# Matmuls of ones in three norm gaps, and late low parts of h in the first product behind a norm

## The chip, the cores and the metric

The kernel runs on one core of one Trainium2 chip. The metric is device time in microseconds (us) of one execution; lower is better. Engines are named as in the profile: PE (TensorE matmuls) and PEld (its weight loads), DVE (VectorE), ACT (ScalarE), POOL (GpSimd), SP (SyncE, which issues the DMAs). The granted clock of TensorE stands at one of two levels, 2.4 GHz (a granted share of 1.0) and 1.2 GHz (0.5); a stretch that saw both shows a value between.

## The reference

A decoder trunk of four layers on x (256 tokens, 1024 features, float32). Each layer has a token mixer (layers 0 and 3 a gated MLP, layer 1 latent attention, layer 2 a gated recurrence) and a convolutional feed-forward part, each behind a norm and a modulation by a conditioning vector:

```python
for i in range(DEPTH):                       # 4
    mod = c_act @ ada_w[i] + ada_b[i]
    sh1, sc1, g1, sh2, sc2, g2 = jnp.split(mod, 6, axis=-1)
    h = modulate(rmsnorm(x, mix_norm_g[i]), sh1, sc1)
    y = mixer(h)                             # by i % 3
    x = x + (1.0 + g1)[:, None, :] * y
    h = modulate(rmsnorm(x, ffn_norm_g[i]), sh2, sc2)
    x = x + (1.0 + g2)[:, None, :] * conv_ffn(h, ff_w_up[i], ...)
return rmsnorm(x, final_g)
```

## The kernel before, in words

Every large product is done with split operands: a weight tile `raw` comes by DMA, ACT casts it to its high part `wh` (L210), DVE subtracts to get the low part `wl` (L213); the activations h are split in the same way into `hh` (cast on ACT, L599) and `hlo` (subtraction on DVE, L600). A product of two such operands is three matmuls (`mm3`, L243 to L245): high by high, high by low, low by high. h lies with features on the partitions, in 8 chunks of 128 features (the K chunks) by 256 tokens.

A *unit* is one weight tile of 1 MB. The up-projection of a feed-forward part (`ffn`) has 22 units, each a `proj_pair`: two output blocks g of 128 features, 8 K chunks, three matmuls of 256 columns each, so 48 matmuls. The first unit behind a norm is called with `outer=True` (in the ffn for c = 0, in `mla` for the pair `cq`, in `hgrn` for the first `hf`): the loop over K chunks is the outer one, so that the product can start when the first chunk of h is there.

Between two products stands a *norm gap*. The last unit of a product (`out_end`) finishes four accumulators one after the other; `residual` adds each to x (DVE, L522, L523) and squares it (ACT, L525); `root` gives the scale per token; `scaled` multiplies x by it into `gx` (L467 for the first 128 tokens, L469 and L470 for the other 128). Then `turned` transposes `gx` on PE into PSUM tiles `xt` (16 transposes of 128x128, L478), and `modulate_chunk` makes each of the 8 chunks: DVE multiplies and adds into `nt` (L487), ACT casts `hh`, DVE subtracts `hlo`. The order of `gx`'s two halves matters: the transposes of a chunk's first 128 tokens need L467, those of the second need L469.

The gaps are named here by what follows them: ffn 0, MLA (the mixer of layer 1), ffn 1, HGRN (the mixer of layer 2), ffn 2, the mixer of layer 3, ffn 3. In some of them small matmuls `adaps<-adaw,cact` of the conditioning vectors are put on PE (`pace`, `GAPS`, `pacing`).

Float32 matmuls of one 128x128 tile with another stand elsewhere too: the program starts with 12 such matmuls of ones (`warmup`, L1253), and each unit of the gated MLP has four (`sv`, L768: two blocks by two halves of the tokens).

The order on each engine is fixed when the program is built: a scheduler lists the instructions, and can set matmuls of the second unit between those of the first; each engine then works through its list in order, waiting on semaphores. `tc.issue_after(i)` makes an instruction stand behind i in that list.

Of the kernel before, what the change touches and what calls it, by code (L numbers as in the profile page):

```python
# [21 lines left out]
P = 128  # L22
# [4 lines left out]
NRAW = 5  # L27
GAPS = [3, 2, 4, 3, 5, 3, 3, 0]
GAPW = 7
GAPBIG = 4  # L30
LAST = 2
GCH = 6
# [59 lines left out]
def build(ctx, tc, A, out, stages=None):  # L92
    nc = tc.nc
    pe, act, dve, pool = nc.tensor, nc.scalar, nc.vector, nc.gpsimd
# [21 lines left out]
    def acc(name, shape=(P, 512)):  # L116
        return pp.tile(list(shape), F32, tag="acc", name=name, bufs=4)
# [29 lines left out]
    onesw = one.tile([P, P], F32, name="ones")  # L147
# [6 lines left out]
    i = act.activation(cact[:], cin[:], AF.Silu)  # L154
# [18 lines left out]
    state = {"dma": 0, "conv": 0, "use": 0, "ahead": 2, "chain": (), "left": 99, "tag": "raw", "p": 0.0, "d": 0.0, "gap": 0, "rate": {"p": 0.0, "d": 0.0}}  # L173
# [18 lines left out]
    def conv_half():  # L192

        if not halves:
            if state["dma"] == state["conv"]:
                if state["dma"] == len(plan):
                    return
                dma_next()
            raw, n = raws.pop(0)
            ready.append([])  # L200
            halves.extend((raw, o, min(1024, n - o), state["conv"]) for o in range(0, n, 1024))
            state["conv"] += 1
        raw, o, w, n = halves.pop(0)
        wh = wp.tile([P, 1024], F32R, tag="wh", name=f"wh{n}_{o}", bufs=5)
        wl = wp.tile([P, 1024], F32R, tag="wl", name=f"wl{n}_{o}", bufs=5)
        with contextlib.ExitStack() as es:

            for ins in state["chain"]:
                es.enter_context(tc.issue_after(ins))
            act.copy(wh[:, :w], raw[:, o : o + w])  # L210
            if "sub1" in state:
                es.enter_context(tc.issue_after(state["sub1"]))
            i = dve.tensor_tensor(wl[:, :w], raw[:, o : o + w], wh[:, :w].bitcast(F32), op=ALU.subtract)  # L213
            state["sub"] = getattr(i, "ins", i)
        ready[-1].append((wh, wl))

    def unit(ahead=None, more=DMA_AHEAD):
        u = state["use"]
        ahead = state["ahead"] if ahead is None else ahead
        while state["dma"] < min(len(plan), u + ahead + (more if u else 0)):  # L220
            dma_next()
        while state["conv"] < min(len(plan), u + ahead) or halves:
            conv_half()
        state["use"] += 1
        r = ready.pop(0)
        pacing()
        return r
# [9 lines left out]
    def hl(parts, o, n):  # L237

        i, r = divmod(o, 1024)
        return parts[i][0][:, r : r + n], parts[i][1][:, r : r + n]  # L240

    def mm3(ps, lh, ll, rh, rl, start, stop):
        pe.matmul(ps, lh, rh, start=start, stop=False)  # L243
        pe.matmul(ps, lh, rl, start=False, stop=False)  # L244
        i = pe.matmul(ps, ll, rh, start=False, stop=stop)  # L245
        state["mm"] = getattr(i, "ins", i)
        return i
# [141 lines left out]
    def ada_load(m):  # L389
        if todo[m]:  # L390
            loaded[m].append((state["use"], todo[m].pop(0)(), state["tag"] == "big"))

    def ada_run(m):
        if not loaded[m]:
            ada_load(m)
        if loaded[m]:
            loaded[m].pop(0)[1]()
            owner[m].pop(0)

    def flush(upto=None, mid=0):  # L400
        for e in list(late):
            if e[0] - mid < state["use"] if upto is None else e[2] <= upto:
                late.remove(e)
                e[1]()

    def need(l, u):

        for m in "pd":
            while owner[m] and min(owner[m]) <= (l, u):
                ada_run(m)  # L410
        flush((l, u))

    def pacing():
# [6 lines left out]
        for m in "pd":  # L420
            while loaded[m] and loaded[m][0][0] + 2 <= state["use"] and not (m == "p" and left <= GAPW):
                ada_run(m)
        for m in "pd":
            if left > (GAPW if m == "p" else 2):
                state[m] += state["rate"][m]
                while state[m] >= 1:
                    state[m] -= 1
                    ada_load(m)
        if left <= GAPW and len(loaded["p"]) < state["gap"]:
            tag, state["tag"] = state["tag"], "big" if sum(e[2] for e in loaded["p"]) < GAPBIG else "raw"  # L430
            ada_load("p")
# [38 lines left out]
        i = act.activation(xn[:, 512:D], x[:, t, 512:D], AF.Copy, scale=rs)  # L470
        state["chain"] += (getattr(i, "ins", i),)

    def turned(c, w, bank=misc):

        ps = bank("xt", (P, w, S))
        for e in range(w):
            for t in range(2):
                pe.transpose(ps[:, e, t * P : t * P + P], cur["gx"][:, t, (c + e) * P : (c + e) * P + P], ident[:])  # L478
        return ps
# [4 lines left out]
    def modulate_chunk(l, which, c, xt):  # L484
        b = 24 * which + c
        t = t1("nt")
        i = dve.tensor_scalar(t[:], xt, amul[:, l, which, c : c + 1], mod[:, l, b : b + 1], op0=ALU.mult, op1=ALU.add)  # L487
        h, lo = split(hh[:, c, :], hlo[:, c, :], t[:])
        return getattr(i, "ins", i), h

    def modulated(l, which):
        tiles = [(0, 1), (1, 2), (3, 2), (5, 2), (7, 1)]

        late = misc if which == 0 and l % 3 == 0 else acc
        xts = [turned(*i) for i in tiles[:3]]
        while loaded["p"]:
            ada_run("p")
        need(l, 1 + 3 * which)
        for i, (c0, w) in enumerate(tiles):
            if 0 < i < 3:  # L500
                xts.append(turned(*tiles[i + 2], late))
            for c in range(c0, c0 + w):
                ins = modulate_chunk(l, which, c, xts[i][:, c - c0, :])
                if c < 2:
                    state["chain"] += ins
                if c in CONVAT:
                    conv_half()
# [111 lines left out]
    def proj_pair(src_h, src_l, nk, name, outer=False):  # L619

        w = unit()
        ps = acc(name, (P, 2, S))
        if outer:
            for k in range(nk):
                for g in range(2):
                    a, b = hl(w, (g * nk + k) * P, P)
                    mm3(ps[:, g, :], a, b, src_h(k), src_l(k), k == 0 and g == 0, k == nk - 1 and g == 1)
            return ps
        for g in range(2):
            for k in range(nk):  # L630
                a, b = hl(w, (g * nk + k) * P, P)
                mm3(ps[:, g, :], a, b, src_h(k), src_l(k), k == 0, k == nk - 1)
            if g == 0:
                flush(mid=1)
        return ps
# [183 lines left out]
    def mla(l):  # L819
# [3 lines left out]
        qr = tables.pop()  # L823
        kr, cs, sn = (qr[:, i, :] for i in (4, 5, 6))
        ps_q = proj_pair(hk, lk, KC, "cq", KOUT > 0)
        cq = t2("cq", (P, 2, S))
        act.copy(cq[:], ps_q[:])
# [440 lines left out]
    for kind, l in stages:  # L1268
# [3 lines left out]
        if kind == "mix":  # L1272
# [3 lines left out]
            if l % 3 == 0:  # L1276
                if quick:
# [4 lines left out]
                    def start(chunk):  # L1282
                        for step in FIRST.split():
                            if step == "d":
                                dma_next()
                                continue
                            if step == "p":
                                with tc.issue_after(state["lastdma"]):
                                    nc.sync.dma_start(prm[:, n0:n1], A["prm"][:, n0:n1])
                                conv_load(l)  # L1290
                                late_c()
                                continue
                            c = int(step[1])
                            if step[0] == "a":
                                if c % 2 == 0:
                                    xt[0] = turned(c, 2)
                                if c:
                                    ada_first(l, c)
                                first_store(l, c)
                                state.setdefault("sub1", modulate_chunk(l, 0, c, xt[0][:, c % 2, :])[0])  # L1300
                            else:
                                chunk(c)

                    gmlp(l, l // 3, start)
                else:
                    modulated(l, 0)
                    gmlp(l, l // 3)
            elif l == 1:
                modulated(l, 0)
                mla(l)  # L1310
            else:
                modulated(l, 0)
                hgrn(l)
# [99 lines left out]
```

## Time and profile before

| | us |
|---|---|
| median of three runs (1352.07 to 1353.33) | 1353.07 |
| the profiled execution | 1353.27 |
| its span, first to last instruction | 1351.2 |
| PE busy | 1316.6 |
| DVE busy | 1112.7 |
| ACT busy | 773.5 |
| mean granted clock of TensorE | 0.993 |

The profiled execution spent 2.07 us outside its span. The profile lists when each instruction started, how long it took, and what ended the idle time before it. Matmuls overlap: each row lasts longer than the distance to the next row, and the distance is the price.

### The profile page before, as it was taken

The page shows a single profiled execution, that of the slowest core. Times are in us where ns is not written, and L with a number is a line of the kernel's source. Part 1 is how long each engine was busy: PE and PEld are TensorE (multiplying, and loading weights), DVE is VectorE, ACT ScalarE, POOL GpSimd, SP SyncE. Part 2 cuts the span into 40 slices and gives each one's busy share as a digit, 9 for nine tenths or more (in the row PEclk, how much of TensorE's full clock was granted, in tenths as well). Part 3 has the DMA queues.
Part 4 walks back from the last instruction along what each step waited for, and adds up shares of the span by engine and source line. Part 5 has one row for each costly group of instructions (what it writes and reads, how often), then busy time and mean ns, then how long its engine had stood idle before and what let it go on. Part 6 is the DMA issues. An engine that isn't in the chain of part 4 may idle for free.

```text
span 1351.2 us, 24627 instructions
## 1 busy us (share of the span) xinstructions
PE 1316.6 (97%) x10092; PEld 1192.5 (88%) x10092; DVE 1112.7 (82%) x1818; ACT 773.5 (57%) x1212; POOL 17.3 (1%) x27
## 2 busy tenths in 40 slices
PE   8999989999989999999999999999999999999997
PEld 6799789998777799998897879999878998899986
DVE  5699788888888789999889988988985964888854
ACT  3764366665366566654675647665455644666643
POOL 0100000000000000000000000000001000000000
PEclk8999999999999999999999999999999999999999
DMA  9868945557986466498675575558977445254550
GB/s 378 349 235 318 403 185 187 213 193 267 424 333 244 172 219 244 166 360 359 236 295 190 219 305 189 214 192 317 369 297 259 168 166 216 98 204 179 198 197 32
DMA packets 49160, 330.68 MB, mean 245 GB/s; under 512 B 6548, under 2 KB 7572, under 8 KB 10134
## 3 DMA queue, kind: packets, MB, share of 16 engines
q1 hardware_dynamic: 47888, 327.40, 63.7%
q10 hardware_dynamic: 1160, 1.71, 0.4%
q8 instruction: 79, 1.29, 0.4%
q14 instruction: 33, 0.27, 0.1%
HBM read 328.01 MB, written 1.08 MB: 244 GB/s over the span
## 4 chain that ended last, share of the span: by engine, by line
PE 85%; DVE 9%; ACT 3%; issue 1%; DMA 1%; ACTq 0%; DVEq 0%
PE up L245 12%; PE up L243 12%; PE up L244 12%; PE dn L243 5%; PE dn L245 5%; PE dn L244 5%; PE u L244 2%; PE u L243 2%; PE u L245 2%; DVE wl L213 2%; PE v L243 2%; PE v L244 2%; PE v L245 2%; PE go L243 2%; PE go L244 2%; PE go L245 2%
## 5 line engine op out<-in xcount | busy, mean ns | idle before, releaser
L210 ACT CAST wh<-raw 128x1024 fp32r<-128x1024 f32 x418 | 432.8, 1048 | 324.0 <-PE up L244 110.9
L213 DVE TENSOR_TENSOR wl<-raw,wh 128x1024 fp32r<-128x1024 f32 x418 | 507.2, 1225 | 84.6 <-ACT wh L210 83.8
L245 PE MATMUL up<-hh,wl 128*128 128x256 f32 x1408 | 397.8, 283 | 0.9 <-DVE wl L213 0.9
L243 PE MATMUL up<-hh,wh 128*128 128x256 f32 x1408 | 397.7, 284 | 0.0
L244 PE MATMUL up<-hlo,wh 128*128 128x256 f32 x1408 | 397.3, 283 | 0.1
L245 PEld LDWEIGHTS up<-hh,wl 128*128 128x128 f32 x1408 | 270.4, 192 | 1.3 <-DVE wl L213 1.3
L243 PEld LDWEIGHTS up<-hh,wh 128*128 128x128 f32 x1408 | 270.0, 192 | 0.6 <-issue 0.4
L244 PEld LDWEIGHTS up<-hlo,wh 128*128 128x128 f32 x1408 | 270.1, 192 | 0.3 <-DVE hlo L600 0.3
L349 DVE CUSTOM_DVE_ANT_0 adaw<-adaw,cbc,prm 128x1024 f32<-128x1024 f32 x120 | 151.3, 1282 | 0.3 <-DMA adaw<-adad 0.3
L244 PE MATMUL dn<-wl,gh 128*128 128x512 f32 x352 | 137.0, 389 | 0.0
L245 PE MATMUL dn<-wh,gl 128*128 128x512 f32 x352 | 136.8, 389 | 0.0
L243 PE MATMUL dn<-wh,gh 128*128 128x512 f32 x352 | 134.7, 390 | 0.5 <-DVE y L1217 0.5
L1215 ACT ACTIVATE y<-up,cwb 128x256 f32<-128x256 f32 x176 | 99.0, 562 | 58.1 <-DVE y L1217 57.9
L1216 DVE SCALAR_TENSOR_TENSOR y<-up,cwb,y 128x255 f32<-128x255 f32 x176 | 84.5, 480 | 34.0 <-ACT y L1215 33.5
L1217 DVE SCALAR_TENSOR_TENSOR y<-up,cwb,y 128x254 f32<-128x254 f32 x176 | 84.1, 478 | 1.5
L243 PEld LDWEIGHTS dn<-wh,gh 128*128 128x128 f32 x352 | 66.0, 188 | 15.2 <-issue 1.7
L245 PEld LDWEIGHTS dn<-wh,gl 128*128 128x128 f32 x352 | 66.1, 188 | 13.7
L244 PEld LDWEIGHTS dn<-wl,gh 128*128 128x128 f32 x352 | 66.1, 188 | 13.5
L243 PE MATMUL u<-hh,wh 128*128 128x256 f32 x256 | 74.0, 289 | 0.0
L245 PE MATMUL u<-hh,wl 128*128 128x256 f32 x256 | 72.4, 283 | 0.0
L244 PE MATMUL u<-hlo,wh 128*128 128x256 f32 x256 | 72.4, 283 | 0.0
L600 DVE TENSOR_TENSOR gl<-g,gh 128x256 fp32r<-128x256 f32 x88 | 37.1, 421 | 22.1 <-ACT gh L599 20.5
(332 smaller groups left out, 2060.4 us busy)
## 6 DMA issues: line engine op xcount, KB each, us to landing
raw<-up SPq DMA_DIRECT2D x88, 1024.0 KB
adaw<-adad SPq DMA_DIRECT2D x60, 1024.0 KB
raw<-dn SPq DMA_DIRECT2D x44, 1024.0 KB
adaw<-adap SPq DMA_DIRECT2D x28, 1024.0 KB
raw<-gmu SPq DMA_DIRECT2D x16, 1024.0 KB
raw<-gmo SPq DMA_DIRECT2D x16, 1024.0 KB
raw<-gmv SPq DMA_DIRECT2D x15, 1024.0 KB
adaf<-ada SPq DMA_DIRECT2D x8, 1024.0 KB
```

Source lines behind the costliest of these rows:

```text
L210: act.copy(wh[:, :w], raw[:, o : o + w])
L213: i = dve.tensor_tensor(wl[:, :w], raw[:, o : o + w], wh[:, :w].bitcast(F32), op=ALU.subtract)
L243: pe.matmul(ps, lh, rh, start=start, stop=False)
L244: pe.matmul(ps, lh, rl, start=False, stop=False)
L245: i = pe.matmul(ps, ll, rh, start=False, stop=stop)
L349: r = dve.tensor_tensor_reduce(raw[:, e, :], raw[:, e, :], cbc[:], 1.0, prm[:, c0 : c0 + 1], ALU.mult, ALU.add, mod[:, l, b : b + 1])
L600: b = dve.tensor_tensor(lo, src, h.bitcast(F32), op=ALU.subtract)
L1215: act.activation(y[:], ps[:, e, :], AF.Identity, bias=b, scale=w[2])
L1216: dve.scalar_tensor_tensor(y[:, 1:], ps[:, e, : S - 1], w[1], y[:, 1:], op0=ALU.mult, op1=ALU.add)
L1217: dve.scalar_tensor_tensor(y[:, 2:], ps[:, e, : S - 2], w[0], y[:, 2:], op0=ALU.mult, op1=ALU.add)
```

## The change

Two edits. First, `turned` gets a parameter `fill`: ahead of the transposes of the first tile it issues that many plain matmuls of a 128x128 tile of ones with itself (float32), into the PSUM tile that the transposes then overwrite, and held behind the last matmul of the product (`state["mm"]`). `modulated` asks for 30 in the gap of ffn 0, 30 in that of MLA, 24 in that of ffn 3, none elsewhere. Second, in the first unit behind a norm the matmuls with `hlo` of a K chunk are issued two K chunks later than those with `hh`. No arithmetic on the data is added or dropped.

```diff
+FILL = [30, 30, 0, 0, 0, 0, 24]
...
-    def turned(c, w, bank=misc):
+    def turned(c, w, bank=misc, fill=0):
+
         ps = bank("xt", (P, w, S))
+        with contextlib.ExitStack() as es:
+            if fill:
+                es.enter_context(tc.issue_after(state["mm"]))
+            for i in range(fill):
+                pe.matmul(ps[:, 0, :P], onesw[:], onesw[:], start=True, stop=True)
...
-        xts = [turned(*i) for i in tiles[:3]]
+        xts = [turned(*i, fill=0 if j else FILL[2 * l + which - 1]) for j, i in enumerate(tiles[:3])]
...
         if outer:
-            for k in range(nk):
-                for g in range(2):
+            for k in range(nk + 2):
+                for g in range(2) if k < nk else ():
                     a, b = hl(w, (g * nk + k) * P, P)
-                    mm3(ps[:, g, :], a, b, src_h(k), src_l(k), k == 0 and g == 0, k == nk - 1 and g == 1)
+                    pe.matmul(ps[:, g, :], a, src_h(k), start=k == 0 and g == 0, stop=False)
+                    pe.matmul(ps[:, g, :], b, src_h(k), start=False, stop=False)
+                for g in range(2) if k > 1 else ():
+                    a = hl(w, (g * nk + k - 2) * P, P)[0]
+                    i = pe.matmul(ps[:, g, :], a, src_l(k - 2), start=False, stop=k == nk + 1 and g == 1)
+            state["mm"] = getattr(i, "ins", i)
             return ps
```

On PE, in the gap of ffn 0, this stood before: the end of the product `go`, the transposes, the first unit.

```order
L244 MATMUL go_1503<-wl_1024_1739,yh_868 128x512
L245 MATMUL go_1503<-wh_1024_1738,yl_869 128x512
L478 MATMUL xt<-ident,gx 128x128 x16
L243 MATMUL up_1931<-hh,wh_0_1759 128x256
L244 MATMUL up_1931<-hlo,wh_0_1759 128x256
```

And this stands there now (the lines of the file have moved by a few):

```order
L245 MATMUL go_1503<-wl_1024_1739,yh_868 128x512
L246 MATMUL go_1503<-wh_1024_1738,yl_869 128x512
L482 MATMUL xt<-ones 128x128 x30
L485 MATMUL xt<-ident,gx 128x128 x16
L635 MATMUL up_1961<-hh,wh_0_1759 128x256
L636 MATMUL up_1961<-hh,wl_0_1760 128x256
```

The 30 matmuls stand between the product and all 16 transposes, so no transpose can run before the last of them. The gaps of MLA (x30) and ffn 3 (x24) read the same.

On PE, the beginning of ffn 1, whose gap has no matmuls of ones, before (`up_5090` is the first unit, `up_5162` the second; `wh_0` and `wh_1024` are the two output blocks of a unit):

```order
L243 MATMUL up_5090<-hh,wh_0_4933 128x256
L244 MATMUL up_5090<-hlo,wh_0_4933 128x256
L245 MATMUL up_5090<-hh,wl_0_4934 128x256
...
L243 MATMUL up_5090<-hh,wh_0_4933 128x256
L243 MATMUL up_5162<-hh,wh_0_5058 128x256
L244 MATMUL up_5162<-hlo,wh_0_5058 128x256
L245 MATMUL up_5162<-hh,wl_0_5059 128x256
```

And now (`up_5150` is the first unit, `up_5222` the second):

```order
L635 MATMUL up_5150<-hh,wh_1024_4997 128x256
L636 MATMUL up_5150<-hh,wl_1024_4998 128x256
L244 MATMUL up_5222<-hh,wh_0_5118 128x256
L245 MATMUL up_5222<-hlo,wh_0_5118 128x256
L635 MATMUL up_5150<-hh,wh_0_4993 128x256
L636 MATMUL up_5150<-hh,wl_0_4994 128x256
L635 MATMUL up_5150<-hh,wh_1024_4997 128x256
L636 MATMUL up_5150<-hh,wl_1024_4998 128x256
L639 MATMUL up_5150<-hlo,wh_0_4993 128x256
L639 MATMUL up_5150<-hlo,wh_1024_4997 128x256
L246 MATMUL up_5222<-hh,wl_0_5119 128x256
```

The second unit's first two matmuls now stand behind 8 matmuls of the first unit (two chunks by two blocks by two) instead of 13; its third one, with `wl`, stands as the 17th in place of the 16th. The lists of ffn 0, ffn 3 and HGRN begin in this same order. On ACT and DVE the order in the norm gaps and through the first unit is as before.

On PE, in the first unit behind the MLA gap, the matmuls of a conditioning tile have moved up (before, one of them stood behind `ckv`'s first two, and the others far behind):

```order
L325 MATMUL adaps<-adaw_2_2_4144,cact 32x256
L635 MATMUL cq<-hh,wh_0_3961 128x256
L636 MATMUL cq<-hh,wl_0_3962 128x256
L635 MATMUL cq<-hh,wh_1024_3965 128x256
L636 MATMUL cq<-hh,wl_1024_3966 128x256
L639 MATMUL cq<-hlo,wh_0_3961 128x256
L639 MATMUL cq<-hlo,wh_1024_3965 128x256
L244 MATMUL ckv<-hh,wh_0_4118 128x256
L245 MATMUL ckv<-hlo,wh_0_4118 128x256
L325 MATMUL adaps<-adaw_2_2_4144,cact 32x256 x4
```

Four of them now stand inside the first unit that stood behind it. Further back in MLA the matmuls of the attention heads and of its output product, and DVE's and ACT's work for them, are interleaved in another order, with the same instructions.

## Rows read from the trace of the kernel before

**Rows 1.** The page, part 1: busy us, share of the span, instructions.
```profile
PE 1316.6 (97%) x10092; PEld 1192.5 (88%) x10092; DVE 1112.7 (82%) x1818; ACT 773.5 (57%) x1212; POOL 17.3 (1%) x27
```

**Rows 2.** Windows by norm gap: length, busy by engine, clock, DMA share, GB/s.
```profile
176.60:180.25 3.65, 3.21 (x16) 2.98 (x17) 2.71 (x7) 2.27 (x5) 0.00 (x0) 0.62 0.00 0
375.00:378.70 3.70, 3.30 (x17) 3.01 (x17) 2.74 (x8) 2.32 (x5) 0.00 (x0) 0.56 1.01 425
464.50:466.80 2.30, 2.15 (x17) 1.72 (x17) 1.67 (x5) 1.26 (x4) 0.00 (x0) 1.00 0.00 0
...
1150.70:1156.05 5.35, 2.99 (x17) 2.75 (x17) 3.54 (x9) 2.68 (x7) 0.00 (x0) 0.78 0.01 3
```

**Rows 3.** Timeline of the gap of ffn 0: start, length, what, idle before.
```profile
172.18 0.39 PE L244 MATMUL go<-wl,yh 128*128 128x512 f32 x1
...
172.40 0.39 PE L245 MATMUL go<-wh,yl 128*128 128x512 f32 x1
...
176.64 0.55 PE L478 MATMUL xt<-ident,gx 128*128 128x128 f32 x3 [3.85 <-DVE gx L467]
...
177.58 3.04 PE L478 MATMUL xt<-ident,gx 128*128 128x128 f32 x13 [0.39 <-DVE gx L469]
178.10 1.19 DVE L487 TENSOR_SCALAR nt<-xt,amul,mod 128x256 f32<-128x256 f32 x2 [0.57 <-PE xt L478]
...
180.27 0.56 PE L243 MATMUL up<-hh,wh 128*128 128x256 f32 x1
```

**Rows 4.** Float32 matmuls of 128x128: timeline; by tile (ns min/median/max, first and last start).
```profile
84.22 1.05 PE L768 MATMUL sv<-wsp,v 128*128 128x128 f32 x8
...
L768 PE MATMUL sv<-wsp,v x128: 272/275/377, 77.4 to 1106.6; 128*128 128x128 f32 x128
...
L1253 PE MATMUL warmup<-ones x24: 421/421/579, 1.1 to 6.1; 128*128 128x128 f32 x24
```

**Rows 5.** Timeline of the gap of ffn 3.
```profile
1150.03 0.39 PE L245 MATMUL go<-wh,yl 128*128 128x512 f32 x1
...
1153.79 2.61 PE L478 MATMUL xt<-ident,gx 128*128 128x128 f32 x11 [2.36 <-DVE gx L469]
1154.30 1.19 DVE L487 TENSOR_SCALAR nt<-xt,amul,mod 128x256 f32<-128x256 f32 x2 [0.57 <-PE xt L478]
```

**Rows 6.** Timeline of the beginning of ffn 1.
```profile
465.76 0.99 DVE L487 TENSOR_SCALAR nt<-xt,amul,mod 128x256 f32<-128x256 f32 x2 [0.42 <-PE xt L478]
...
466.79 0.38 PE L243 MATMUL up<-hh,wh 128*128 128x256 f32 x1
467.10 1.04 ACT L210 CAST wh<-raw 128x1024 fp32r<-128x1024 f32 x1
...
468.36 1.22 DVE L213 TENSOR_TENSOR wl<-raw,wh 128x1024 fp32r<-128x1024 f32 x1
...
469.63 0.38 PE L245 MATMUL up<-hh,wl 128*128 128x256 f32 x1 [0.37 <-DVE wl L213]
469.85 0.28 PE L243 MATMUL up<-hh,wh 128*128 128x256 f32 x1
```

**Rows 7.** Windows on matmuls of `up`: the first 62 of three ffns.
```profile
180.25:187.94 7.69, 7.67 (x62) 0.96 0.09 14
466.78:475.24 8.46, 8.00 (x62) 1.00 0.01 2
1156.03:1163.89 7.86, 7.85 (x62) 0.93 0.00 1
```

**Rows 8.** Timeline of the gap of MLA.
```profile
370.98 0.39 PE L245 MATMUL dn<-wh,gl 128*128 128x512 f32 x1
...
376.52 1.18 DVE L487 TENSOR_SCALAR nt<-xt,amul,mod 128x256 f32<-128x256 f32 x2 [0.57 <-PE xt L478]
```

**Rows 9.** MLA: timeline of conditioning matmuls; window of PE over the stage.
```profile
393.15 1.48 PE L324 MATMUL adaps<-adaw,cact 128*32 128x256 f32 x24
...
379.00:464.00 85.00, 84.71 (x653) 1.00 0.67 260
```

## The prediction

> **What bounds the kernel now.** I read the page first. PE is busy for 1316.6 of 1351.2 us, and DVE for 82% of the span [rows 1]. So a change pays or costs where PE stands still or runs slowly, and both edits touch such places, the norm gaps. The windows over the gaps are the second view. Here the reader is to look at the clock: in the gaps of ffn 0, MLA and ffn 3 the granted clock is 0.62, 0.56 and 0.78, so it was at 1.2 GHz for most or part of the stretch; in that of ffn 1 it is 1.00 [rows 2]. Third, the timeline of such a gap says what PE did before the clock fell. In ffn 0 it stood idle for 3.85 us until `gx` was there [rows 3]; in ffn 3 for 2.36 us [rows 5]. The price of the low clock stands in the same rows: in ffn 0 thirteen transposes start between 177.58 and 180.27, where `up` follows them, so they are 2.69 / 13 = 0.21 us apart; rows of that shape at full clock are 0.11 us apart (below).
>
> But the transposes do not stand alone on the path. Behind the first of them DVE makes `nt`, ACT `hh`, DVE `hlo`, chunk after chunk, and PE's first unit follows that chain. In ffn 0 `nt` starts at 178.10 and PE resumes at 180.27 [rows 3]; in ffn 1, at full clock, at 465.76 and 466.79 [rows 6]. To compare gaps I count how far PE has come: 62 matmuls of `up` have started by 187.93 in ffn 0, 475.23 in ffn 1, 1163.88 in ffn 3 (each window ends 0.01 us behind the 62nd start) [rows 7]. From the first `nt` that is 9.83, 9.47 and 9.58 us. So a gap that fell to the low clock loses only 0.1 to 0.4 us in this stretch against one that did not: DVE's chain hides most of it. There is little for the ones to win.
>
> **What the ones cost.** The trace before has no matmul of ones in a gap, but it has the same operation elsewhere. `sv` is a float32 matmul of 128x128; four of them make 8 rows, which last 1.05 us, one row 0.275, so the rows are (1.05 - 0.275) / 7 = 0.111 us apart, and one matmul, two rows, takes 0.222 us [rows 4]. The warm-up agrees on the two rows: 12 matmuls of ones are 24 rows there too, from 1.1 to 6.1, 5.0 / 23 = 0.22 us apart, twice as far, at the start of the program [rows 4]. So 30 matmuls take 60 x 0.111 = 6.66 us, and 24 take 5.33 us. They stand ahead of all 16 transposes, and what is queued behind them on PE is everything else.
>
> *ffn 0.* Products start 0.22 us apart and the last one starts at 172.40 [rows 3], so the ones begin at 172.62 and end at 179.28. `gx` had been ready in both halves by 177.58: the transposes now wait about 1.7 us for PE itself. The first chunk needs the first and third transpose (in the built list one of the next chunk stands between them): the third starts 2 x 0.11 us behind the first, lasts about 0.27 us like the rows of `sv`, and DVE starts 0.04 us after it, so `nt` starts at 179.28 + 0.53 = 179.81, which is 1.71 us later than before.
>
> *ffn 3.* The last product starts at 1150.03 [rows 5]; ones from 1150.25 to 1155.58. In the new list the second transpose completes the first chunk here, 0.11 us sooner: `nt` at 1155.58 + 0.42 = 1156.00 in place of 1154.30, 1.70 us later.
>
> *MLA.* The last product starts at 370.98 [rows 8]; ones from 371.20 to 377.86; `nt` at 378.39 in place of 376.52, 1.87 us later.
>
> **What PE makes of it, and the late low parts.** For the stretch behind `nt` I take ffn 1, which has a full clock and in which the second edit alone acts, and set the new list of PE against the times of its inputs. Matmuls there are 0.12 us apart, and 0.22 us behind one that waited. Before, the second matmul had to wait for `hlo` at once, and the 16th, with `wl`, until 469.63 [rows 6]. In the new list 8 matmuls with `hh` run from 466.79 to 467.85. Then the second unit's first matmul needs `wh`, done at 467.10 + 1.04 = 468.14: it starts at 468.19, the next at 468.41. Four with the third chunk and two with `hlo` follow from 468.53, and the 17th wants `wl`, done at 468.36 + 1.22 = 469.58: it starts at 469.63, where the 16th did [rows 6]. The 18th starts at 469.85, none waits behind it, and the 62nd starts 44 x 0.12 = 5.28 us later, at 475.13: 0.10 us earlier than before, 9.37 us behind `nt`. So the wait for `hlo` goes, and the wait for the weight casts, which stand behind the chunks on ACT and DVE, takes its place. HGRN begins in the same order; I give it 0.10 too. In ffn 2, whose conditioning matmuls lie in the gap, I count nothing.
>
> With 9.37 us behind `nt` the 62nd matmul starts at 189.18 in ffn 0, **1.25 us later** than before, and at 1165.37 in ffn 3, **1.49 us later**. For MLA, whose list is like that of ffn 0, I let it win back the same 1.71 - 1.25 = 0.46 us: 1.41 late, less four conditioning matmuls that now run inside this stretch. At 24 rows in 1.48 us they are 8 rows of 0.06 us, some 0.5 us, and PE is busy for 84.71 of 85.00 us in this stage, so work done earlier is saved later [rows 9]: **0.95 us**. The new interleaving of the attention heads I take as nothing: with 0.29 us idle it can win that much at most, and new waits could cost perhaps 0.5.
>
> Sum: 1.25 + 1.49 + 0.95 - 0.10 - 0.10 = +3.5 us. Almost no wait elsewhere could absorb it, PE being busy for 97% of the span [rows 1]. On the profiled execution's own 1353.27 that is 1356.8; it ran 0.2 us above the median, so I say 1353.07 + 3.5 = **1356.6**.
>
> Bounds. From above, `nt`'s whole lateness arrives, if DVE and ACT alone set the stretch: 1.71 + 1.70 + 1.87 = 5.3 us, 1358.4. From below only PE's own lateness counts. The 16 transposes take 16 x 0.11 = 1.76 us, so PE resumes at 181.04 in ffn 0, 0.77 us late, and saves some 0.4 us there that its first matmuls lost at the low clock; by the same count 0.8 us remain in ffn 3 and 0.5 in MLA. That makes 0.4 + 0.8 + 0.5 - 0.2 = 1.5 us, 1354.6. I choose near the middle, since before the change both bounds were close to being met at once.
>
> **Rivals.** *The ones fit the wait (not slower).* If a matmul of ones took one row's time, 0.111 us, they would end at 175.95 in ffn 0 and 1152.91 in ffn 3, before `gx`. `nt` would stand where it stands, the clock would stay up, and 9.37 us behind 178.10 and 1154.30 the 62nd would start 0.46 and 0.21 us earlier; with 0.4 for MLA and 0.2 for the late low parts that is -1.3 us, 1351.8. It decides at a fill that ends 0.53 (0.42) us before 187.93 - 9.37 = 178.56 and 1163.88 - 9.37 = 1154.51: after 5.41 us, 24 matmuls, in ffn 0, and 3.84 us, 17 matmuls, in ffn 3. Against it speak the two rows per matmul in both places of [rows 4].
>
> *The clock falls all the same, in the transposes.* Then 16 of them take 0.21 instead of 0.11 us each, 1.6 us per gap. PE would resume at 182.6 in ffn 0 with its data ready, and the 62nd would start 7.3 us later, at 189.96, 0.8 us behind the forecast; three times that gives 1359.0. The Trainium skill, "TensorE: Matmul & The Clock Gate", Part 4, says that a transpose does not count as busy for the clock in the way of other matmuls; by that rule this would be the case. The trace speaks against it: the clock fell behind idle time, and in ffn 1 it stayed at 1.00 through all the transposes [rows 2].
>
> *The lateness is won back in the units behind the gap.* DVE is idle for 18% of the span, so its lateness against PE can go, but PE's own can't. If the waits on weight casts vanished, 1353.5.
>
> **Chances.** The forecast, between its bounds, 0.75; the ones fit 0.10; won back 0.09; the clock falls 0.06. A measurement of this kernel can tell about 0.2%, 2.7 us, from no change. Of the forecast's 0.75 I put 0.62 above +2.7 us and 0.13 below; the rival with the clock adds 0.06 to slower. Of the fit, 0.05 is faster by more than 0.2% (gaps that won all of 0.4 us and more), the rest no change; won back is no change. That makes faster 0.05, same 0.27, slower 0.68. The range reaches from 1353.5, where the won-back case begins, to 1358.4, the upper bound; outside lie the fit and the falling clock.
>
> **What would show it.** Right: 60, 60 and 48 rows of ones in the three gaps; granted clock 1.00 there; the first `nt` 1.7 to 1.9 us later behind the last product, with DVE waiting for PE; 62 matmuls in about 9.4 us behind `nt`; in ffn 1 a wait for `wh` ahead of the one for `wl`. Wrong: ones half as long, a clock under 1.00 in a gap, or PE idle in MLA's attention by much more than 0.29 us.

## The result, and the profile after

The changed kernel takes 1357.09 us (median of 9 runs, 1355.15 to 1358.22) against 1353.33 us for the kernel before in the same session (9 runs, 1351.96 to 1354.07). The ratio is 1.0028, 95% interval [1.0018, 1.0037]: slower by 0.28%, 3.8 us. The profiled execution took 1355.59 us, its span is 1353.7 us.

The page, part 1, of the kernel after (busy us, share of the span, instructions):

```profile
PE 1328.3 (98%) x10260; PEld 1207.0 (89%) x10260; DVE 1112.8 (82%) x1818; ACT 772.9 (57%) x1212; POOL 17.3 (1%) x27
```

PE has 168 rows more than in [rows 1], which are the 60, 60 and 48 rows of ones (each float32 matmul makes two rows); DVE, ACT and POOL have the instructions that they had.

The windows over the gaps of ffn 0, MLA, ffn 1 and ffn 3, from the end of the product to the transposes or, in ffn 1, to the first matmul of `up` (length, busy by engine, granted clock, DMA share, GB/s):

```profile
171.62:178.31 6.69, 6.69 (x61) 6.69 (x60) 4.53 (x10) 4.42 (x11) 0.00 (x0) 1.00 0.70 294
371.50:378.20 6.70, 6.70 (x62) 6.70 (x60) 4.39 (x11) 4.31 (x11) 0.00 (x0) 1.00 1.02 427
462.88:467.76 4.88, 4.60 (x55) 2.90 (x54) 4.11 (x11) 3.40 (x11) 0.00 (x0) 1.00 0.00 0
1151.22:1156.58 5.36, 5.36 (x50) 5.36 (x49) 2.33 (x6) 2.18 (x6) 0.00 (x0) 1.00 0.01 3
```

The granted clock is 1.00 in all of them, 2.4 GHz, where [rows 2] had 0.62, 0.56 and 0.78. PE is busy for the whole of each filled gap. The timeline of the gap of ffn 0, which answers to [rows 3], shows with what:

```profile
171.39 0.39 PE L246 MATMUL go<-wh,yl 128*128 128x512 f32 x1
...
171.62 6.86 PE L482 MATMUL xt<-ones 128*128 128x128 f32 x60
...
176.02 0.72 ACT L471 ACTIVATE gx<-x,ss 128x512 f32<-128x512 f32 x1 [0.23 <-DVE ss L460]
176.03 0.49 DVE L470 TENSOR_SCALAR gx<-x,ss 128x512 f32<-128x512 f32 x1
...
178.31 1.91 PE L485 MATMUL xt<-ident,gx 128*128 128x128 f32 x16
178.84 1.00 DVE L494 TENSOR_SCALAR nt<-xt,amul,mod 128x256 f32<-128x256 f32 x2 [2.33 <-PE xt L485]
...
179.98 0.36 PE L635 MATMUL up<-hh,wh 128*128 128x256 f32 x1
```

`gx` is complete at 176.02 + 0.72 = 176.74. The first transpose starts at 178.31, behind the last of the ones, and DVE stands idle for 2.33 us until PE has made the first chunk. It was the other way round in [rows 3], where PE waited 3.85 us for DVE. The gap of ffn 3, for [rows 5], reads the same:

```profile
1150.99 0.39 PE L246 MATMUL go<-wh,yl 128*128 128x512 f32 x1
...
1151.22 5.52 PE L482 MATMUL xt<-ones 128*128 128x128 f32 x48
...
1157.00 1.00 DVE L494 TENSOR_SCALAR nt<-xt,amul,mod 128x256 f32<-128x256 f32 x2 [2.30 <-PE xt L485]
```

The windows on the first 62 matmuls of `up` in ffn 0, 1 and 3, for [rows 7]:

```profile
179.97:188.22 8.25, 7.99 (x62) 1.00 0.00 1
467.75:476.11 8.36, 8.00 (x62) 1.00 0.01 2
1158.23:1166.38 8.15, 7.99 (x62) 1.00 0.00 1
```

In ffn 0 the 62nd starts at 188.21, 9.37 us behind `nt`; in ffn 3 at 1166.37, 9.37 us behind `nt` again. The beginning of ffn 1, for [rows 6]:

```profile
467.76 0.39 PE L635 MATMUL up<-hh,wh 128*128 128x256 f32 x1
...
469.17 0.38 PE L244 MATMUL up<-hh,wh 128*128 128x256 f32 x1 [0.19 <-ACT wh L211]
...
470.60 0.39 PE L246 MATMUL up<-hh,wl 128*128 128x256 f32 x1 [0.16 <-DVE wl L214]
```

Eight matmuls run without a wait. Then PE waits for `wh` of the second unit, later for its `wl`.

**Where the time went.** The next table holds, for each kernel that was profiled, its stages less those of the kernel before, in us. The stages are cut where PE starts the last matmul of a product ahead of a norm, or the 62nd matmul behind one. "To ffn 0" is the program up to ffn 0's gap; "ffn 0" and "ffn 3" run from the last product ahead of the gap to the 62nd matmul of `up`; "MLA" from the last product ahead of it to the last product ahead of ffn 1; "ffn 1" from there to the 62nd matmul; "HGRN" from the last product ahead of it to that ahead of ffn 2; "ffn 2 on" from there to ffn 3's gap. The stretches that are left differ by 0.07 us at most.

| kernel | to ffn 0 | ffn 0 | MLA | ffn 1 | HGRN | ffn 2 on | ffn 3 | span |
|---|---|---|---|---|---|---|---|---|
| before, us | 172.40 | 15.53 | 90.71 | 13.54 | 151.67 | 343.63 | 13.85 | 1351.24 |
| after | -1.01 | +1.29 | +0.67 | -0.09 | +0.11 | -0.03 | +1.52 | +2.46 |
| e1_no_ones | -0.44 | -0.04 | -0.58 | -0.09 | +0.21 | -0.03 | +0.05 | -0.89 |
| e2_ones_only | +0.45 | +1.41 | +0.95 | 0.00 | +1.46 | -0.03 | +1.64 | +5.96 |
| e3_short | -1.44 | -0.38 | +0.61 | -0.11 | +2.85 | -0.04 | -0.37 | +1.10 |
| e4_long | -1.26 | +4.54 | +4.63 | -0.09 | +1.72 | 0.00 | +4.19 | +13.68 |
| e5_shift_early | -0.40 | -0.61 | -0.30 | -0.10 | +2.59 | 0.00 | +0.20 | +1.34 |
| e6_short_shift | -0.97 | +1.00 | +0.61 | -0.09 | +0.43 | +0.01 | -0.36 | +0.61 |
| e7_two_gaps | +0.76 | -0.39 | -0.17 | -0.10 | +0.13 | -0.01 | -0.35 | -0.13 |
| e8_shift_late | +0.47 | +0.05 | -0.33 | -0.10 | -0.07 | -0.05 | -0.36 | -0.43 |
| e9_small_ones | -0.41 | -0.10 | -0.87 | -0.10 | -0.09 | -0.01 | -0.36 | -1.97 |
| e10_small_more | +0.18 | -0.61 | -0.18 | -0.09 | +1.11 | -0.06 | -0.37 | -0.09 |

The change's loss lies in the three filled gaps: 1.29 + 0.67 + 1.52 = 3.48 us, and stays to the end. The first column has nothing to do with the edits: the clock at the start of the program differs from one execution to the next. Between 6 and 20 us the mean granted clock is 0.76 in the execution of before, and 0.88 in that of after (before, then after):

```profile
6.00:20.00 14.00, 9.31 (x175) 7.06 (x178) 7.29 (x19) 5.48 (x10) 0.00 (x0) 0.76 1.02 414
...
6.00:20.00 14.00, 9.41 (x215) 7.59 (x216) 8.46 (x23) 5.67 (x11) 0.00 (x0) 0.88 1.02 411
```

So the profiled execution of after gained 1.01 us by luck, and the two spans differ by only 2.46 us where the medians differ by 3.8.

### The profile page after: what moved, and what is told of

Same layout as the page of the kernel before. It is cut to its first block, busy times and chain, and to the rows that moved or that the text cites. A ratio compares the mean times of both kernels' runs of the same rounds, so it can differ in the third digit from the quotient of the medians.

```text
span 1353.7 us, 24963 instructions
## 1 busy us (share of the span) xinstructions
PE 1328.3 (98%) x10260; PEld 1207.0 (89%) x10260; DVE 1112.8 (82%) x1818; ACT 772.9 (57%) x1212; POOL 17.3 (1%) x27
## 3 DMA queue, kind: packets, MB, share of 16 engines
q8 instruction: 80, 1.31, 0.4%
q10 hardware_dynamic: 1160, 1.71, 0.4%
## 4 chain that ended last, share of the span: by engine, by line
PE 58%; DVE 8%; ACT 2%; issue 1%; ACTq 0%; DVEq 0%
PE up L246 8%; PE up L245 8%; PE up L244 8%; PE dn L244 4%; PE dn L245 4%; PE dn L246 4%; DVE wl L214 2%; PE go L246 1%; PE go L245 1%; PE go L244 1%; PE v L244 1%; PE v L246 1%; PE v L245 1%; PE wo L244 1%; PE u L245 1%; PE u L244 1%
## 5 line engine op out<-in xcount | busy, mean ns | idle before, releaser
L246 PE MATMUL up<-hh,wl 128*128 128x256 f32 x1344 | 380.6, 283 | 1.0 <-DVE wl L214 0.7
L244 PE MATMUL up<-hh,wh 128*128 128x256 f32 x1344 | 380.7, 283 | 0.3 <-ACT wh L211 0.2
L245 PE MATMUL up<-hlo,wh 128*128 128x256 f32 x1344 | 380.3, 283 | 0.0
L246 PEld LDWEIGHTS up<-hh,wl 128*128 128x128 f32 x1344 | 257.9, 192 | 1.8 <-DVE wl L214 1.8
L244 PEld LDWEIGHTS up<-hh,wh 128*128 128x128 f32 x1344 | 258.0, 192 | 1.3 <-ACT wh L211 0.9
L245 PEld LDWEIGHTS up<-hlo,wh 128*128 128x128 f32 x1344 | 258.0, 192 | 0.0
```

## The experiments

Each kernel was run beside the kernel before on the same chip, in three sessions on three chips: e1 to e4 (before took 1353.51 us there), e5 to e8 (1353.55) and e9 and e10 (1352.62). So medians are compared within a session, and ratios across sessions.

**First set: the two edits apart, and the size of the fill.** *e1_no_ones* keeps the late low parts and leaves the ones out:

```diff
-FILL = [30, 30, 0, 0, 0, 0, 24]
+FILL = [0, 0, 0, 0, 0, 0, 0]
```

> The late low parts alone, no matmuls of ones. Theory (the ones outlast the wait for gx, and that is the whole cost): the clock falls again in the gaps of ffn 0, MLA and ffn 3; in ffn 1 and HGRN the 62nd matmul of the first units comes 0.1 us earlier behind nt than before, in all -0.2 to -0.5 us, no difference that the timing shows. Rival (the late low parts and the new interleaving behind them cost, the ones only fill idle time): +2 to +3.5 us.

It took 1352.44 us (10 runs); the ratio to before is 0.9994 [0.9984, 1.0004]. Late low parts by themselves cost nothing that shows, so the rival falls that the new order of the first unit is what is slow. By the table this kernel wins 0.09 us in ffn 1 and 0.58 in MLA; by a count told below, with e7_two_gaps, the 0.58 has another cause.

*e2_ones_only* has the ones and before's order of the first unit:

```diff
-            for k in range(nk + 2):
-                for g in range(2) if k < nk else ():
+            for k in range(nk):
+                for g in range(2):
...
+                    mm3(ps[:, g, :], a, b, src_h(k), src_l(k), k == 0 and g == 0, k == nk - 1 and g == 1)
```

> The ones alone (30, 30, 24), low parts in their old place. Theory: +3.7 us, since the 0.1 us of ffn 1 and HGRN are missing; from the last product to the 62nd matmul of up about 16.9 us in ffn 0, as with both edits or up to 0.2 more. Rival (late low parts and interleaving cost): within 1 us of the kernel before.

It took 1358.47 us (4 runs), ratio 1.0039 [1.0024, 1.0054]. That is 5.0 us above before, where 3.7 were expected. The loss comes with the ones alone: 1.41, 0.95 and 1.64 us in the three gaps, 4.0 in all; the profile has 1.46 us more in HGRN, which the sum did not have.

*e3_short* has fewer ones, so that they end before `gx` is ready, by the break-even points of the prediction (24 and 17):

```diff
-FILL = [30, 30, 0, 0, 0, 0, 24]
+FILL = [21, 21, 0, 0, 0, 0, 15]
```

> Both edits, with 21, 21 and 15 matmuls of ones, which at 0.222 us each end after 4.66 and 3.33 us, just ahead of the second half of gx in all three gaps. Theory: granted clock 1.00 in the gaps, nt where it stood before (within 0.2 us), 62nd matmul 0.5 us earlier than before in ffn 0 and 0.2 in ffn 3, in all -1.0 to -1.5 us. Rival 1 (each one costs its time wherever it stands): 0.7 of the +3.5, so +2.4 us. Rival 2 (ones that end ahead of the transposes do not hold the clock): clock under 1.00 in the gaps, -0.2 to +0.3 us.

It took 1355.39 us (10 runs), ratio 1.0014 [1.0005, 1.0023]: a miss. The total, +1.9 us, lies near the +2.4 of the rival in which each matmul costs its time wherever it stands. Yet in ffn 0 and ffn 3 it did what the theory expected, 0.38 and 0.37 us faster than before (0.5 and 0.2 were said), with the clock at 1.00, so that rival falls. The loss is in HGRN, 2.85 us, where this kernel has no ones; and MLA lost 0.61.

*e4_long* has more of them:

```diff
-FILL = [30, 30, 0, 0, 0, 0, 24]
+FILL = [45, 45, 0, 0, 0, 0, 36]
```

> Both edits, with half as many ones again: 45, 45 and 36. Theory: all of what is added lies on the path, 2 x 3.33 + 2.66 = 9.3 us more than the change, so +12.8 us against the kernel before; from the last product to nt 10.7 us in ffn 0. Rival (DVE's and ACT's chain hides part of it): +9 us or less.

It took 1367.98 us (2 runs), ratio 1.0109 [1.0088, 1.0129]. Against the kernel after, ffn 0 lost 3.25 us more for 15 more matmuls and ffn 3 lost 2.67 for 12 more. That is 0.217 and 0.222 us each, the price per matmul of the prediction, all of it on the path. The kernel as a whole lost 14.5 us against before, where 12.8 were expected: HGRN lost 1.72 us here too, and MLA 3.96 more than in the kernel after, for 15 matmuls that cost 3.33.

**What happens in HGRN.** All the profiles so far, that of before too, have one thing in common there. In the `gram` matmuls, rows of 128x32 that follow each other about 0.009 us apart, PE stands idle for a while that the profile puts down to `issue`, that is, to no wait that it can show. In e3_short it is longest (timeline, then the windows ahead of and behind the point where the clock fell):

```profile
735.22 0.32 PE L1065 MATMUL gram<-qk 128*32 128x32 f32 x12 [2.43 <-issue]
...
732.20:735.60 3.40, 0.97 (x83) 0.82 (x70) 2.15 (x4) 1.06 (x1) 0.00 (x0) 1.00 0.02 5
735.79:739.20 3.41, 3.41 (x18) 3.41 (x17) 3.41 (x4) 0.55 (x1) 0.00 (x0) 0.50 0.02 5
```

The same row of the kernel before, and of the kernel after:

```profile
734.88 0.70 PE L1052 MATMUL gram<-qk 128*32 128x32 f32 x56 [1.06 <-issue]
...
735.96 0.63 PE L1065 MATMUL gram<-qk 128*32 128x32 f32 x49 [1.29 <-issue]
```

In e3_short the clock stands at 0.50, 1.2 GHz, behind 2.43 us of idle PE. The idle stretch itself is 1.1 us longer than in the kernel after, whose clock stays at 1.00 here. Why is it longer? Count PE's rows from the start of the program. PE resumes at row 5584 in the kernel before, at 5712 in e2_ones_only, e3_short and the kernel after, at 5968 in e4_long (to one row, since records can be missing): all 128 apart or a multiple of it. The page has the queue that fits, here that of the kernel after (packets, MB, share):

```profile
q8 instruction: 80, 1.31, 0.4%
```

1.31 MB in 80 packets are 16 KB each. PE has 10260 matmuls and as many weight loads, 20520 / 80 = 256 to a packet, 128 rows of matmuls with their loads: the packets are PE's own instructions. And by their times in the trace, PE resumes 1.38 us behind the landing of such a packet in the kernel before (landed at 733.51), 1.46 in the kernel after (734.50), 1.49 in e3_short (733.73). The Trainium skill, "Runtime: NRT & Kernel Launch", section "Instruction fetch mechanics", says that an engine's instructions come in blocks of 16 KiB, 256 instructions; the packets agree. It adds that crossing from one to the next is mostly hidden; in `gram`, where 128 rows are used up in about 2.25 us, these rows show that it is not.

So my theory became: rows added ahead of HGRN move `gram` against the 128-row steps, the idle stretch changes with the place, and where it is long the clock falls behind it. The rival: the fall is chance, or it follows from the clock kept up in the earlier gaps.

**Second set: the place in the instruction stream.** These kernels use a second kind of ones, of 32x32, that adds rows at little time:

```diff
-            for i in range(fill):
+            for i in range(fill[0]):
+                pe.matmul(ps[:32, 0, :32], onesw[:, :32], onesw[:, :32], start=True, stop=True)
+            for i in range(fill[1]):
                 pe.matmul(ps[:, 0, :P], onesw[:], onesw[:], start=True, stop=True)
```

with a pair (of 32x32, of 128x128) for each gap. *e5_shift_early* moves HGRN by the 84 rows of e3_short, and *e8_shift_late* puts the same 84 rows behind HGRN (`Z` is a gap without ones):

```diff
+FILL = [(42, 0), Z, Z, Z, Z, Z, Z]          # e5_shift_early
+FILL = [Z, Z, Z, Z, Z, Z, (42, 0)]          # e8_shift_late
```

> The late low parts alone, as in e1 (1352.4 us), and 42 matmuls of ones of 32x32 (84 rows of PE) in the gap of ffn 0, where PE stands idle for 3.85 us anyway; nothing keeps the clock up there. Theory of the place in the instruction stream: the idle stretch of PE in HGRN's gram matmuls ends 1.3 to 1.5 us behind the landing of a 16 KB instruction packet, and stands at rows of PE that are 128 apart, so 84 rows ahead of HGRN move it to the place that it has in e3_short. It then lasts 2.2 to 2.6 us in place of 1.4, the clock falls behind it, and the kernel takes 1353.5 to 1355.4 us. Rival, that the clock falls in HGRN because it was kept up in the gaps, or by chance: idle stretch 1.4 us, 1352.4 us within 0.5.

> As e5_shift_early, with the 42 matmuls of 32x32 in the gap of ffn 3, behind HGRN. Theory of the place: HGRN as in e1, 1352.4 us within 0.5. If the 84 rows cost something by themselves, or by where they put the stages behind them, it shows here too: 1353 us or more.

e5_shift_early took 1355.37 us (11 runs), ratio 1.0014 [1.0005, 1.0022]; e8_shift_late 1352.46 us (11 runs), ratio 0.9992 [0.9983, 1.0001]. They have the same instructions, 84 rows in another place, and differ by 2.9 us. The rows of `gram`, and the window behind the fall, of e5_shift_early:

```profile
735.08 0.32 PE L1067 MATMUL gram<-qk 128*32 128x32 f32 x13 [2.42 <-issue]
...
736.63:740.04 3.41, 3.41 (x70) 3.19 (x72) 3.41 (x4) 1.06 (x1) 0.00 (x0) 0.50 0.02 5
```

and of e8_shift_late:

```profile
734.83 0.46 PE L1067 MATMUL gram<-qk 128*32 128x32 f32 x32 [1.04 <-issue]
...
735.00:738.40 3.40, 3.40 (x91) 3.23 (x86) 3.40 (x4) 0.06 (x1) 0.00 (x0) 1.00 0.02 5
```

2.42 us of idle against 1.04, a clock of 0.50 against 1.00, HGRN 2.59 us longer against 0.07 shorter. So the place decides over the idle stretch. One rival is still open at this point: the small ones kept the clock up in the gap of ffn 0 of e5_shift_early (1.00 from 172.30 to 178.35, which I had not expected), so the fall in HGRN could follow from that; e6, e7 and e10, below, answer it. The fall may not come in every execution: the eleven of e5_shift_early spread from 1352.11 to 1357.09 us, wider than those of any kernel here, but only one was profiled.

*e6_short_shift* and *e7_two_gaps* start from e3_short and bring the rows ahead of HGRN to 128, so that it stands to the steps as in the kernel before:

```diff
+FILL = [(24, 19), (0, 21), Z, Z, Z, Z, (0, 15)]   # e6_short_shift
+FILL = [(0, 21), (43, 0), Z, Z, Z, Z, (0, 15)]    # e7_two_gaps
```

> e3_short (1355.4 us) with two of the ones in ffn 0 replaced by 24 of 32x32, so that 128 rows of PE are added ahead of HGRN in place of 84, in the same time. Theory of the place in the instruction stream: HGRN stands to the 128-row steps as in the kernel before, the idle stretch in gram is 1.0 to 1.5 us instead of 2.4, the stage takes 151.7 to 152.3 us from last product to last product instead of 154.5, and the kernel 1352.3 to 1353.8 us. Rival, that the short ones or the kept-up clock cost it: 1355.4 us within 0.5.

> e3_short with MLA's 21 ones replaced by 43 of 32x32, which take about 1 us of a gap of 3.7 us: 128 rows ahead of HGRN, the clock kept up in ffn 0 and ffn 3 alone. Theory of the place: HGRN as in the kernel before (151.7 to 152.3 us), ffn 0 and ffn 3 each 0.4 us better than before, MLA within 0.7 us of before: 1351.5 to 1353.0 us. Rival, that the short ones cost it: some two thirds of e3_short's loss stay, 1354.5 us or more.

e6_short_shift took 1354.99 us (11 runs), ratio 1.0015 [1.0006, 1.0024]: the total is a miss, and lies where the rival had it. HGRN did as the theory says, 152.10 us with 1.56 us idle in `gram` (1.0 to 1.5 were said) and no fall of the clock, in place of 154.52 and 2.43. But ffn 0 lost 1.00 us where e3_short had won 0.38, because I had mis-sized the 32x32 ones. I took them at 0.011 us per row, as I had sized the rows of `gram`. The timelines have this, of 128 rows of `gram` in e10_small_more and of the gap in e5_shift_early:

```profile
737.22 1.30 PE L1067 MATMUL gram<-qk 128*32 128x32 f32 x128
...
172.32 2.85 PE L482 MATMUL xt<-ones 128*32 128x32 f32 x84
```

One row lasts 0.20 us, so those of `gram` are (1.30 - 0.20) / 127 = 0.009 us apart. The 84th of the ones starts at 174.97, so they are (174.97 - 172.32) / 83 = 0.032 us apart. So in e6_short_shift 48 of them took 48 x 0.032 = 1.5 us, where the two matmuls of 128x128 that they replace take 0.44: most of the 1.38 us by which the two kernels differ in ffn 0.

e7_two_gaps took 1352.24 us (11 runs), ratio 0.9991 [0.9982, 1.0000], inside what was expected. HGRN stands 0.13 us from before, ffn 0 and ffn 3 won 0.39 and 0.35. It differs from e3_short only in MLA's ones, so the two show what 43 small ones in place of 21 matmuls of 128x128 are worth: by the profiles 2.85 - 0.13 = 2.72 us in HGRN, which the rows of the small ones put back in place, and 0.78 us in MLA (0.61 against -0.17). And the clock was up in all three gaps of e7_two_gaps, as in e3_short and e6_short_shift, yet it did not fall in HGRN: that part of the rival falls.

What is left of MLA's differences lies in its conditioning matmuls. Each kernel has 106 rows of them in that stage, but the scheduler groups them otherwise, and a group of two rows lasts as long as one of eight (e3_short):

```profile
374.72 0.62 PE L325 MATMUL adaps<-adaw,cact 128*32 128x256 f32 x2
...
377.81 0.64 PE L325 MATMUL adaps<-adaw,cact 128*32 128x256 f32 x8
```

The group of two stands between the transposes and holds them up by 0.55 us; e6, e7 and e10 have it too (two rows, not four as I wrote ahead of e10). Taken from each group's start to the next matmul, without idle time, the 106 rows take 8.27 us in these four kernels, 7.92 in the kernel before, 7.60 in the kernel after, and 7.32 in e1, e5, e8 and e9. The last is 0.60 us less than before, as much as e1_no_ones won in the whole stage (0.58): by this count it is the scheduler's grouping that won there, and not the late low parts as such.

**Third set: ones that fit.** *e9_small_ones* and *e10_small_more* use 32x32 ones alone:

```diff
+FILL = [(32, 0), (32, 0), Z, Z, Z, Z, (32, 0)]   # e9_small_ones
+FILL = [(42, 0), (42, 0), Z, Z, Z, Z, (32, 0)]   # e10_small_more
```

> The late low parts, and 32 matmuls of ones of 32x32 in each of the three gaps: 64 rows 0.0325 us apart (as e5 and e7 measured them), 2.1 us, so they end well before gx; 128 rows ahead of HGRN, which so stands to the 128-row steps as before. Theory (ones that fit the wait win what the transposes lose at 1.2 GHz; the place in the stream sets HGRN): clock up in all three gaps, the 62nd matmul 14.9 us behind the last product in ffn 0 (15.53 before, 14.92 in e5) and 13.5 in ffn 3 (13.85 before, 13.49 in e8), MLA's stage 0.3 better than in e1, gram's idle stretch 1.0 to 1.6 us; in all 1.0 to 1.3 us under e1's 1352.44: 1351.1 to 1351.5 us. Rival, that so short a fill does not hold the clock: 1352.4 us.

> As e9 with 42, 42 and 32 of them: 168 rows ahead of HGRN, 40 behind a 128-row step of before, a place that no run has shown. The gaps as in e9 (within 0.2 us; in MLA four conditioning rows stand between the transposes, which may cost 0.4). Theory of the place: gram's idle stretch differs from e9's by over 0.3 us or stands at another row, and the time follows it, by 0.5 us or more in either direction; if it does not, the place matters only at some positions. Rival (the place is nothing, e5 was chance): within 0.4 us of e9.

e9_small_ones took 1351.38 us (11 runs; before, in the same session, 1352.62), ratio 0.9990 [0.9981, 0.9999]. That is 1.24 us under before, less than the 0.2% that a measurement can tell, and inside the range that was named. But the range was reckoned from e1's 1352.44 us, of another session. Against before of their own sessions e1_no_ones was 1.07 us faster, e8_shift_late 1.09 and e7_two_gaps 1.31, so the times do not show that small ones win anything over no ones. The profiles do: outside the start of the program e9_small_ones is 1.56 us shorter than before, and e1_no_ones 0.45, one execution each. In that of e9_small_ones the clock fell in ffn 0 all the same, at 176.81, behind 1.71 us of idle PE, and the 62nd matmul came 15.43 us behind the last product, where 14.9 was expected. MLA (-0.87) and ffn 3 (-0.36) held it, as expected; in MLA PE had stood idle for 1.56 us (the first transposes in ffn 0 and in MLA):

```profile
176.23 0.55 PE L487 MATMUL xt<-ident,gx 128*128 128x128 f32 x3 [1.71 <-DVE gx L468]
...
374.57 0.55 PE L487 MATMUL xt<-ident,gx 128*128 128x128 f32 x3 [1.56 <-DVE gx L468]
```

e10_small_more took 1353.02 us (11 runs), ratio 1.0002 [0.9993, 1.0011]. Its three gaps won 1.16 us in all (0.61, 0.18 and 0.37; those of e9_small_ones 1.33), but HGRN lost 1.11 us, with the idle time in more than one place:

```profile
733.44 1.03 PE L1067 MATMUL gram<-qk 128*32 128x32 f32 x96 [0.79 <-issue]
...
740.61 0.28 PE L245 MATMUL hg<-hlo,wh 128*128 128x256 f32 x1 [0.82 <-issue]
...
746.65 0.44 PE L1067 MATMUL gram<-qk 128*32 128x32 f32 x27 [1.67 <-issue]
```

The same stretch of e9_small_ones has 1.03 us in `gram` and 0.63 in `hg`. At 40 rows behind a step the place costs 1.2 us of HGRN without any fall of the clock; that agrees with the theory, and e9's 1.6 us lead is what was named as its sign. What the best place is was not tried.

Why the place sets the length can be read off the traces, though no run tested it. At the first of these stops in each of the twelve profiles, the 128 rows ahead of it are all `gram`, or all but three, and take 2.2 to 2.3 us. The 128 rows before those took 3.6 to 4.0 us in e3_short, e4_long and e5_shift_early, which then stood idle for 2.17 to 2.43 us, and 11.7 us or more in the other nine, which stood idle for 0.79 to 1.56. PE stops for long where it has used up two blocks of instructions fast, one behind the other.

## Why the prediction was right

It said 1356.6 us, with 1353.5 to 1358.4 as its range, and slower by +3.5; measured were 1357.09 and +3.8. The mechanism held: the ones outlast the wait, `nt` comes late by what they outlast it, and PE wins part of that back behind `nt`. That the stages of the profile add up to the forecast so closely (+3.47 without the start of the program) is in part luck: the sum had MLA 0.28 us too high and HGRN 0.21 too low. By its own steps:

- **The price of the ones** held. The 60 rows of ffn 0 fill 171.62 to 178.31, 6.69 us for the 6.66 of the sum; the 48 rows of ffn 3 fill 5.36 for 5.33. e4_long confirms it from the other side. The rival in which they take half as long, and fit the wait, is out.
- **`nt` is late** by what was worked out. Behind the last product it starts 7.45 us later in ffn 0 (5.70 in [rows 3]), 6.01 in ffn 3 (4.27 in [rows 5]) and 7.45 in MLA (from 371.28 to 378.73; 5.54 in [rows 8]): 1.75, 1.74 and 1.91 us for 1.71, 1.70 and 1.87.
- **9.37 us to the 62nd matmul**, taken from ffn 1 alone, is what ffn 0, ffn 1 and ffn 3 all show. This step did the work: it turned 1.7 us of lateness into +1.29 in ffn 0 and +1.52 in ffn 3 (1.25 and 1.49 in the sum), since at the full clock the stretch behind `nt` is 0.46 and 0.21 us shorter than in [rows 7].
- **The late low parts** came out in ffn 1, -0.09 for -0.10, with the wait for `wh` ahead of that for `wl`. In HGRN's beginning too the 62nd matmul comes 0.09 us sooner behind the product.
- **MLA** was mis-sized: +0.67 for the 0.95 of the sum. At the last matmul of `ckv` PE is 1.58 us later behind the last product than before (22.13 for 20.55), where the sum had 1.41. Of that 0.91 is won back by the end of the stage, where the sum had 0.46 for the four conditioning matmuls that moved up; the eight rows that now stand ahead of `ckv`'s last account for 0.57 of it, and the rest lies in the stage behind, whose new order was taken as nothing.
- **The clock** stays at 1.00 through the gaps and through the 16 transposes behind them (178.31 to 179.95). The rival in which it falls in the transposes did not come, nor in e4_long's longer gaps. The Trainium skill's rule from "TensorE: Matmul & The Clock Gate", Part 4, that a transpose doesn't count as busy in the way of other matmuls, did not decide anything here: these 16 transposes, 1.64 us of them, ran at 1.00.
- **Won back later** it was not: from the 62nd matmul behind ffn 0 to MLA's gap the two kernels differ by 0.01 us, behind that of ffn 3 by 0.03.
- **Not in the prediction** was HGRN. In the profiled execution of after it costs 0.11 us, where the sum counted on a win of 0.10. e2_ones_only has the same 120 rows ahead of HGRN, and there the clock fell once behind 1.52 us of idle PE and HGRN cost 1.46. Whether such falls are among the executions of the kernel after that took over 1357.5 us is open: only one of them was profiled.

The break-even points, 24 and 17 matmuls, were right for the gaps they were worked out for: carried back from the kernel after at e4_long's prices they are 30 - 1.29 / 0.217 = 24.1 and 24 - 1.52 / 0.222 = 17.2, and e3_short wins there. They would have been a wrong forecast for the kernel: the gaps are not the only place that a longer instruction list reaches.

## What to carry to other kernels

Before you fill a wait to hold the clock, ask what the low clock costs behind it: here the chain on DVE hid most of it. Fills that ended in time and held the clock won 0.38 to 0.61 us in ffn 0 and 0.35 to 0.37 in ffn 3 by the profiles (the prediction had 0.46 and 0.21), and each 0.22 us matmul beyond the wait was paid in full. If you fill, let the ones end before the data come, and look at the clock: in the profiled executions 42 small ones held it in ffn 0 and 32 did not. And instructions added in one place move every fast stretch behind them against the steps in which PE's instructions arrive: compare the stages that you did not touch, with the same rows put behind them as a control.

## What the runs showed of the hardware that was not expected

- PE waits for its own instructions. Where rows are about 0.009 us apart (`gram`), it stood idle for 0.79 to 2.43 us at rows 128 apart, and resumed 1.26 to 1.5 us behind the landing of a 16 KB instruction packet. Moving HGRN by 84 rows cost 2.9 us; by 128 rows the stage changed by 0.43 us at most.
- In these profiles the clock fell to 1.2 GHz behind idle stretches of PE of 1.52 to 2.43 us in `gram` in four kernels, and stayed up behind 0.79 to 1.67 us there in the others. The two ranges overlap, so the length of the stretch alone does not decide.
- The price of a small matmul of ones is not that of another of its shape: rows of 128x32 were 0.032 us apart for ones that all write one PSUM place, and about 0.009 us apart in `gram`, whose matmuls write four groups of 32 partitions in turn. Which of the differences makes it was not tried.
- A group of two conditioning rows (one matmul) took 0.55 us to the next matmul and a group of eight (four matmuls, which write four groups of 32 partitions) 0.57. By how the scheduler grouped them, MLA's 106 rows took from 7.32 to 8.27 us.
- The start of the program differs between executions by up to 2.2 us (the first column of the table, -1.44 to +0.76), more than most of the effects told here.
